# Writing a small transposed table to memory: 2048 four-byte pieces, or a turn on TensorE and 16 rows

## The chip, the cores and the metric

The kernel runs on one core of a Trainium2 chip. The metric is device time in microseconds (us) of one execution. Five engines work in parallel, each through its own list of instructions in order: TensorE (PE in the profile), VectorE (DVE), ScalarE (ACT), GpSimd (POOL) and SyncE (SP), which here issues most of the DMA transfers.

## The reference

Two layers of a diffusion backbone work on 512 latent tokens and 256 context tokens of 1024 channels, in 32-bit floats. A layer normalises its input, modulates it by a shift and a scale that depend on a conditioning vector, projects it, runs two attentions side by side (a neighbourhood attention and a grouped-query attention, 8 heads of 64 each), merges them through gates, projects once more, and adds the result to its input, multiplied by a third conditioning factor, the residual gate:

```python
mod_x = jax.nn.silu(c) @ w_ada + b_ada
shift_x, scale_x, gate_x = jnp.split(mod_x[:, None, :], 3, axis=-1)
mod_c = jax.nn.silu(c_ctx) @ w_ada + b_ada
shift_c, scale_c, gate_c = jnp.split(mod_c, 3)
hx = _rmsnorm(x, norm_g) * (1.0 + scale_x) + shift_x
hc = _rmsnorm(ctx, norm_g) * (1.0 + scale_c) + shift_c
...
out_x = _merge(a_att, b_att, a_z, b_z, g_a, g_b, w_o_a, w_o_b, w_out)
x_new = x + gate_x * out_x
if update_ctx:            # layer 0 only
    ...
    ctx = ctx + gate_c * out_c
```

This document is about how the 1024 values of `gate_x` (and, in layer 0, the 1024 of `gate_c`) travel from where they are computed to where they multiply.

## The kernel before

Tokens are worked in tiles of 128. Products are kept close to 32-bit accuracy by splitting both operands in a high and a low part and adding three products (`mm3`, lines 429 to 431: these three lines are most of PE's work). Weights come in as `raw` tiles of 128x512 (lines 397 and 411, issued by SyncE), ScalarE casts them to the high part `whi` (lines 399 and 414), and VectorE or GpSimd subtract to get the low part `wlo` (lines 402 and 416).

A layer goes through these stages: the projections for the neighbourhood attention (pool `cp0` or `cp1`), the neighbourhood attention (`na`), the projections for the grouped-query attention (`bp`), that attention (`gq`), and the merge with the output projection (`mrg`). While attention heads wait for their softmax, PE works on pieces of other projections from a list called `fill`: the paths through SiLU (`za`, lines 610 and 612), the merge gates and the first output projection.

In the grouped-query stage, head by head, `gq_scores` computes four blocks of 128 queries against 768 keys (lines 857 and 858), takes the maximum (VectorE, line 1127) and the exponential (ScalarE, line 1128), and then `turned` (line 795) casts the probabilities to a 16-bit high part `h` on ScalarE (line 798), subtracts for a low part on VectorE or GpSimd (line 799), and has SyncE issue a DMA transpose of both into `ht` (line 800). `gq_values` divides (lines 807 and 808), multiplies `ht` with the values (lines 1144 and 1145, all four blocks of the head at once) and hands the result to `head_out` (lines 791 to 793). `hilo` splits the gated results (lines 652 and 653).

The conditioning factors that are not needed at once are computed in the background, spread over the stages. `ada_steps` loads the weight columns as `rawb` tiles (line 288) and has VectorE form dot products into `asum` (line 295), one column of 128 channels at a time, for each of two halves of the conditioning vector. For the residual gates these are tiles 16 to 23; `gate_steps` (line 589) makes the list of them and puts `ada_gate` at its end. The list is run one step at a time between blocks of attention:

- Layer 0 has two conditioning vectors (latent and context, `nv` = 2). Its first half runs in the neighbourhood attention, its second half, with `ada_gate` at the end, in the grouped-query attention, one step after each block of queries (line 1130).
- Layer 1 has one (`nv` = 1). The whole list runs in the first projections, a few steps after each token tile (lines 735, 747 and 748).

`ada_gate` adds the two halves (line 304, tile `as`) and the bias (line 314, tile `ag`), halves the result (line 316) and stores it to a table in memory, `gd`, from line 317. In SBUF the values lie with the channel inside a block of 128 on the partitions and the block number along the row. In `gd` they lie as rows of 128 channels. At the start of the merge, line 1180 reads each vector back as one row of 1024, spread over all 128 partitions (`gate`), and line 1218 multiplies with it.

The order of the instructions on each engine is written by a planner that simulates the program with costs of its own and takes whatever it thinks is ready; only where `behind` (line 464) is used is an order fixed by hand. `turn` (line 516) and the divisions use the two PSUM buffers of kind `t`. In the attentions, `pool` is the pool of the stage (`att["p"]`; `Parts` puts two named tiles elsewhere), and `hp["p"]` in the projections.

Of the kernel before, what the change touches and what calls it, by code (L numbers as in the profile page):

```python
# [7 lines left out]
F32 = mybir.dt.float32  # L8
# [62 lines left out]
def hybrid_kernel(es: ExitStack, tc, x, ctx, cvec, w_ada, w_ada0, small, gvec, w_in, w_o_a, w_o_b, w_out,  # L71
                  bias_int, bias_edge, rope, ident_d, out):
    nc = tc.nc
    V, S, G, T = nc.vector, nc.scalar, nc.gpsimd, nc.tensor
# [10 lines left out]
    def nm(s):  # L85
        uid[0] += 1
        return f"{s}_{uid[0]}"
# [26 lines left out]
    def psw(n=512, kind="w"):  # L114
        if kind == "w":
            kind = "f" if pm["i"] % pm["n"] == 0 else "x"
            pm["i"] += 1
            if pm["i"] in pm["v_for"]:
                kind = "v"
        pool, cols = pm[kind]  # L120
        return pool.tile([128, cols], F32, tag=kind, name=nm("ps" + kind))[:, :n]
# [5 lines left out]
    gd = [drp.tile([16, 128], F32, name=f"gd{i}") for i in range(2)]  # L127
# [11 lines left out]
    ident = cp.tile([128, 128], F32, name="ident")  # L139
# [136 lines left out]
    def ada_steps(l, tiles, halves, nv, pool, queue=None):  # L276

        cb = {}

        def load(h):  # L280
            cb[h] = pool.tile([128, 2, 512], F32, tag="cb", name=nm("cb"), bufs=1)
            for v in range(nv):
                src = cd[8 * v + 4 * h:8 * v + 4 * h + 4].rearrange("k p -> (k p)").unsqueeze(0)
                nc.sync.dma_start(cb[h][:, v, :], src.to_broadcast([128, 512]))

        def load_tile(h, i):
            cb["w"] = pool.tile([128, 512], F32, tag="rawb", name=nm("rawb"), bufs=2)
            (queue or nc.sync).dma_start(cb["w"], w_ada[l, h, i])

        def dot(h, i, v):  # L290
            if v == 0:
                load_tile(h, i)
            w = cb["w"]
            o = w if v == nv - 1 else pool.tile([128, 512], BF16, tag="junk", name=nm("junk"), bufs=1)
            behind(ON_DVE, lambda: V.tensor_tensor_reduce(o, w, cb[h][:, v, :], 1.0, 0.0, ALU.mult, ALU.add,
                                                          asum[:, i, h, v:v + 1]))
        res = []
        for h in halves:
            res += [lambda h=h: load(h)] + [lambda h=h, i=i, v=v: dot(h, i, v) for i in tiles for v in range(nv)]
        return res  # L300

    def ada_sum(a, b, nv):
        s = sp.tile([128, b - a, 2], F32, tag="as", name=nm("as"), bufs=1)
        V.tensor_tensor(s[:, :, 0:nv], asum[:, a:b, 0, 0:nv], asum[:, a:b, 1, 0:nv], ALU.add)
        return s
# [1 line left out]
    def ada_mod(l):  # L307
        mod_finish(l, ada_sum(0, 16, 2).rearrange("p (a k) v -> p a k v", a=2), 0, 8)

    def ada_gate(l, nv):  # L310

        g = sp.tile([128, 2, 8], F32, tag="ag", name=nm("ag"), bufs=1)
        n = 8 * nv
        V.tensor_tensor(g[:, 0:nv], ada_sum(16, 24, nv)[:, :, 0:nv].rearrange("p k v -> p v k"),
                        gcol[:, 52 + 8 * l:60 + 8 * l].unsqueeze(1).to_broadcast([128, nv, 8]), ALU.add)
        V.tensor_scalar(g[:, 0:nv], g[:, 0:nv], 0.5, None, ALU.mult)
        nc.sync.dma_start(gd[l][0:n].rearrange("n p -> p n"), g[:, 0:nv].rearrange("p v k -> p (v k)"))


    def make_hx(l, t, xt, hx, pool):  # L320
# [259 lines left out]
    def layer(l, hx, nxt, start):  # L580
# [6 lines left out]
        nv = 2 if first else 1  # L587

        def gate_steps(halves, pool):
            return (ada_steps(l, range(16, 24), halves, nv, pool)  # L590
                    + ([lambda: ada_gate(l, nv)] if 1 in halves else []))
        gq = gcol[:, 48 + 2 * l:49 + 2 * l]
        gk = cp.tile([128, 1], F32, name=nm("gk"))

# [121 lines left out]
        else:  # L716
# [3 lines left out]
            for t in range(6):  # L720
                tok_proj(w, 512, a_hx, t, evac_na(kav, False, gk, 4))
            bg = gate_steps((0, 1), hp["p"])
            run(bg, 1)
        per_bg = -(-len(bg) // (3 + qt))
# [30 lines left out]
        if True:  # L755
# [266 lines left out]
            def values_of(dst, f, back=None):  # L1022
# [6 lines left out]
                return g  # L1029

            bg = gate_steps((0,), att["p"]) if first else []
            pipeline(fill, 9, na_first, values_of(za, na_values), bg=bg)

# [127 lines left out]
            def early():  # L1161

                for c in (1, 3):
# [4 lines left out]
            own = {"cb": vbig[:, 1152:2176].rearrange("p (v n) -> p v n", v=2),  # L1168
                   "junk": vbig[:, 2176:2432].bitcast(BF16)}
            bg = gate_steps((1,), Parts(att["p"], own)) if first else []  # L1170
            pipeline(fill, 8, gq_first, values_of(zb, gq_values, vs[:, 1:2]), early, bg)
            gq_es.close()
# [323 lines left out]
```

## Time and profile before

| | us |
|---|---|
| three runs | 1131.86 median, 1130.71 lowest, 1135.87 highest |
| the profiled execution | 1136.54 |
| its span, first to last instruction | 1134.8 |
| PE busy, matmuls | 1092.4 |
| VectorE, ScalarE, GpSimd busy | 765.3, 578.0, 490.5 |
| mean granted clock of PE | 0.989 of full |

The granted clock is the share of PE's full clock that the chip allows at that moment. Views of the profile used below: the page (busy times, and a table of DMA issues by kind with the median time to landing), the list of waits (who waited for whom: total, times, longest, in us), windows (busy time of each engine in a stretch, with clock and DMA rate), the timeline (start, length, engine, line, operation, with the idle time before it and what ended it in brackets), and the chain of work that ended last (start, length, what). An engine with a q behind its name is its instruction sequencer. A line such as L317 is a line of the kernel.

### The profile page before, as it was taken

The page shows a single profiled execution, that of the slowest core. Times are in us where ns is not written, and L with a number is a line of the kernel's source. Part 1 is how long each engine was busy: PE and PEld are TensorE (multiplying, and loading weights), DVE is VectorE, ACT ScalarE, POOL GpSimd, SP SyncE. Part 2 cuts the span into 40 slices and gives each one's busy share as a digit, 9 for nine tenths or more (in the row PEclk, how much of TensorE's full clock was granted, in tenths as well). Part 3 has the DMA queues.
Part 4 walks back from the last instruction along what each step waited for, and adds up shares of the span by engine and source line. Part 5 has one row for each costly group of instructions (what it writes and reads, how often), then busy time and mean ns, then how long its engine had stood idle before and what let it go on. Part 6 is the DMA issues. An engine that isn't in the chain of part 4 may idle for free.

```text
span 1134.8 us, 16867 instructions
## 1 busy us (share of the span) xinstructions
PE 1092.4 (96%) x5824; PEld 905.5 (80%) x5824; DVE 765.3 (67%) x1492; ACT 578.0 (51%) x1152; POOL 490.5 (43%) x405
## 2 busy tenths in 40 slices
PE   8999999999999999779999999999999999999998
PEld 5688888888988877557788888887888987777677
DVE  4666788888365478636567895357988765677473
ACT  6463266656333566555331275325666545776431
POOL 1044255654246245345521454335554563463530
PEclk9999999999999999989999999999999999999999
DMA  9454412233341597679733542453333236989742
GB/s 366 148 173 134 126 49 66 83 125 98 110 140 47 130 205 176 108 216 248 192 104 127 158 149 77 142 182 72 108 105 112 64 103 164 186 219 250 198 147 81
DMA packets 195278, 161.29 MB, mean 142 GB/s; under 512 B 119444, under 2 KB 161144, under 8 KB 193528
## 3 DMA queue, kind: packets, MB, share of 16 engines
q1 hardware_dynamic: 187856, 145.82, 47.2%
q0 software_dynamic: 2368, 7.87, 2.1%
q10 hardware_dynamic: 4968, 6.53, 1.7%
q8 instruction: 46, 0.75, 0.3%
q14 instruction: 40, 0.33, 0.1%
HBM read 115.58 MB, written 17.32 MB: 117 GB/s over the span
## 4 chain that ended last, share of the span: by engine, by line
PE 78%; DMA 6%; DVE 5%; issue 5%; POOL 3%; ACT 2%; SPq 1%; POOLq 0%; ACTq 0%; DVEq 0%
PE psx L431 11%; PE psx L430 11%; PE psx L429 11%; PE psf L429 9%; PE psf L430 8%; PE psf L431 8%; PE pst L775 2%; PE pss L951 2%; PE pss L857 2%; PE pss L858 2%; DMA raw<-in_w_in_dram 2%; DMA ht<-h 1%; PE pst L521 1%; PE pst L1144 1%; PE pst L1145 1%
## 5 line engine op out<-in xcount | busy, mean ns | idle before, releaser
L429 PE MATMUL psf<-hx,whi 128*128 128x512 f32 (+1 forms) x360 | 137.9, 383 | 4.1 <-ACT zt L610 2.5
L416 POOL TENSOR_TENSOR wlo<-raw,whi 128x512 fp32r<-128x512 f32 x70 | 98.0, 1405 | 94.4 <-ACT whi L414 64.3
L431 PE MATMUL psf<-hx,wlo 128*128 128x512 f32 (+1 forms) x360 | 135.8, 377 | 0.0
L430 PE MATMUL psf<-hx,whi 128*128 128x512 f32 (+1 forms) x360 | 135.2, 376 | 0.0
L429 PE MATMUL psx<-whi,hx 128*128 128x512 f32 (+1 forms) x328 | 120.7, 371 | 0.0
L430 PE MATMUL psx<-wlo,hx 128*128 128x512 f32 (+1 forms) x328 | 119.7, 366 | 0.0
L431 PE MATMUL psx<-whi,hx 128*128 128x512 f32 (+1 forms) x328 | 119.5, 365 | 0.0
L414 ACT CAST whi<-raw 128x512 fp32r<-128x512 f32 x136 | 82.5, 620 | 72.6 <-DMA raw<-in_w_in_dram 44.9
L402 POOL TENSOR_TENSOR wlo<-raw,whi 128x512 fp32r<-128x512 f32 x40 | 61.0, 1528 | 120.6 <-ACT whi L399 73.0
L799 POOL TENSOR_TENSOR h<-p,h 128x768 f16<-128x768 f32 (+1 forms) x40 | 64.9, 1626 | 99.7 <-ACT h L798 79.1
L399 ACT CAST whi<-raw 128x512 fp32r<-128x512 f32 x88 | 54.4, 623 | 100.4 <-PE psx L431 33.9
L500 POOL TENSOR_TENSOR ss<-ss,ehalf 128x8 f32<-128x8 f32 (+2 forms) x40 | 62.2, 1558 | 74.1 <-DVE ss L497 74.0
L416 DVE TENSOR_TENSOR wlo<-raw,whi 128x512 fp32r<-128x512 f32 x66 | 66.6, 1009 | 28.9 <-ACT whi L414 27.4
L1127 DVE CUSTOM_DVE_ANT_0 p<-pss,vb 128x768 f32<-128x768 f32 x64 | 60.2, 953 | 36.7 <-PE pss L858 19.9
L429 PEld LDWEIGHTS psf<-hx,whi 128*128 128x128 f32 x360 | 67.9, 189 | 16.1 <-ACT zt L610 3.6
L431 PEld LDWEIGHTS psf<-hx,wlo 128*128 128x128 f32 x360 | 67.8, 188 | 11.5
L430 PEld LDWEIGHTS psf<-hx,whi 128*128 128x128 f32 x360 | 67.9, 189 | 10.3
L1128 ACT ACTIVATE p<-pss,mx 128x768 f32<-128x768 f32 x64 | 57.5, 900 | 35.0 <-DVE mx L1127 31.5
L431 PEld LDWEIGHTS psx<-whi,hx 128*128 128x128 f32 x328 | 61.9, 189 | 10.0
L430 PEld LDWEIGHTS psx<-wlo,hx 128*128 128x128 f32 x328 | 62.0, 189 | 9.2
L429 PEld LDWEIGHTS psx<-whi,hx 128*128 128x128 f32 x328 | 61.7, 189 | 8.9
L429 PE MATMUL psx<-hx,whi 128*128 128x256 f32 (+1 forms) x208 | 68.1, 327 | 0.0
(359 smaller groups left out, 3097.5 us busy)
## 6 DMA issues: line engine op xcount, KB each, us to landing
raw<-in_w_in_dram SPq DMA_DIRECT2D x168, 256.0 KB, 2.9
rawb<-in_w_ada_dram SPq DMA_DIRECT2D x48, 256.0 KB, 2.8
raw<-in_w_out_dram SPq DMA_DIRECT2D x32, 256.0 KB, 3.1
tg<-gs SPq DMA_DIRECT2D x4, 1536.0 KB, 6.4
rawx<-in_w_ada_dram SPq DMA_DIRECT2D x4, 1024.0 KB, 13.3
rawy<-in_w_ada_dram SPq DMA_DIRECT2D x4, 1024.0 KB, 10.3
gs<-zt ACTq DMA_DIRECT2D x16, 256.0 KB, 2.1
raw<-in_w_o_a_dram SPq DMA_DIRECT2D x16, 256.0 KB, 3.4
```

The costliest lines, as they stand in the source:

```text
L399: S.copy(hi[:, :n], raw[:, :n])
L402: e.tensor_tensor(lo[:, :n], raw[:, :n], F(hi[:, :n]), ALU.subtract)
L414: S.copy(hi, raw)
L416: lo_eng(i).tensor_tensor(lo, raw, F(hi), ALU.subtract)
L429: T.matmul(ps, lhs[0], rhs[0], start=first, stop=False)
L430: T.matmul(ps, lhs[0], rhs[1], start=False, stop=False)
L431: T.matmul(ps, lhs[1], rhs[0], start=False, stop=last)
L500: G.tensor_tensor(ss, ss, ehalf[:, :n], ALU.pow)
L775: T.transpose(pt[:, c0:c0 + 128], src, ident)
L799: eng.tensor_tensor(h[:, 1], p[:, :n], h[:, 0], ALU.subtract)
L1127: V.tensor_tensor_reduce(p, pss, lift, -1.0, 3e38, ALU.add, ALU.min, mx[:, 0:1])
L1128: S.activation(p, pss, AF.Exp, bias=mx[:, 0:1], accum_out=r[:, i:i + 1])
```

## The change

Instead of writing `gd` straight from the tile `ag` through a transposed access pattern, in which neighbouring elements in memory come from different partitions (16 x 128 pieces of 4 bytes in layer 0, 8 x 128 in layer 1), `ada_gate` turns the tile on TensorE through a PSUM buffer of kind `t`, copies the 16 (or 8) rows of 128 to a small tile `agt` on ScalarE, and stores those rows, 512 bytes each. `ada_gate` is handed the pool in which `agt` lies.

```diff
-    def ada_gate(l, nv):
+    def ada_gate(l, nv, pool):
 
         g = sp.tile([128, 2, 8], F32, tag="ag", name=nm("ag"), bufs=1)
         n = 8 * nv
         V.tensor_tensor(g[:, 0:nv], ada_sum(16, 24, nv)[:, :, 0:nv].rearrange("p k v -> p v k"),
                         gcol[:, 52 + 8 * l:60 + 8 * l].unsqueeze(1).to_broadcast([128, nv, 8]), ALU.add)
         V.tensor_scalar(g[:, 0:nv], g[:, 0:nv], 0.5, None, ALU.mult)
-        nc.sync.dma_start(gd[l][0:n].rearrange("n p -> p n"), g[:, 0:nv].rearrange("p v k -> p (v k)"))
+        pt = psw(512, "t")
+        T.transpose(pt[0:n, 0:128], g[:, 0:nv].rearrange("p v k -> p (v k)"), ident)
+        gt = pool.tile([16, 128], F32, tag="agt", name=nm("agt"), bufs=1)
+        S.copy(gt[0:n], pt[0:n, 0:128])
+        nc.sync.dma_start(gd[l][0:n], gt[0:n])
...
         def gate_steps(halves, pool):
             return (ada_steps(l, range(16, 24), halves, nv, pool)
-                    + ([lambda: ada_gate(l, nv)] if 1 in halves else []))
+                    + ([lambda: ada_gate(l, nv, pool)] if 1 in halves else []))
```

## Prediction

> **What bounds the kernel now.** I read the page first, for the busiest engine and its idle total; then the list of PE's waits, to see which stall is long; then a table of short windows around that stall; then SyncE's own timeline and the chain of waits through it, for the cause; and last the same places in layer 1.
>
> ```profile
> span 1134.8 us, 16867 instructions
> PE 1092.4 (96%) x5824; PEld 905.5 (80%) x5824; DVE 765.3 (67%) x1492; ACT 578.0 (51%) x1152; POOL 490.5 (43%) x405
> ```
>
> TensorE (PE) is busy for 1092.4 of 1134.8 us. Only PE's 42.4 us of idle time, and time at a reduced clock, can be won without removing matmuls. The profiled execution took 1136.54 us, 1.74 more than its span.
>
> ```profile
> PE pst L1144 <- DMA ht<-h: 14.8, 3, 11.8
> 474.60 0.28 PE L858 MATMUL pss<-gk,qs 128*128 128x256 f32 x1
> 486.71 0.59 PE L1144 MATMUL pst<-ht,vb 128*128 128x512 f16 x1 [11.83 <-DMA ht<-h]
> ```
>
> One wait (total, times, longest, in us) is 11.8 us long: PE stops at 474.88 and resumes at 486.71 because a DMA transpose into `ht` is late. That is over a quarter of PE's idle time, in layer 0's grouped-query stage. The windows there (span, busy us of each engine, granted clock, DMA share, GB/s):
>
> ```profile
> core 0: us, PE busy (x) PEld busy (x) DVE busy (x) ACT busy (x) POOL busy (x), PEclk, DMA share, GB/s
> 465.00:467.00 2.00, 2.00 (x10) 1.68 (x9) 1.20 (x2) 1.95 (x4) 0.00 (x0) 1.00 1.15 299
> 470.00:475.00 5.00, 4.88 (x38) 4.50 (x36) 4.69 (x5) 2.55 (x7) 2.39 (x2) 1.00 0.21 12
> 475.00:477.00 2.00, 0.00 (x0) 0.00 (x0) 0.20 (x3) 0.00 (x0) 0.00 (x0) 1.00 0.16 12
> 479.00:480.00 1.00, 0.00 (x0) 0.00 (x0) 0.00 (x0) 0.00 (x0) 0.00 (x0) 0.66 0.70 119
> 480.00:484.00 4.00, 0.00 (x0) 0.00 (x0) 0.00 (x0) 1.41 (x4) 0.72 (x1) 0.50 1.22 264
> ```
>
> From 470 to 477 the DMA engines move 12 GB/s, then 264 once something has cleared. During the stall VectorE, ScalarE and GpSimd have almost nothing to do either, so the time isn't being used for something else that would be late next. PE's clock falls to half at about 479.3 (0.66 over that one microsecond), 4.4 us after PE stopped. SyncE (SPq) shows what the queue holds:
>
> ```profile
> 464.93 0.37 SPq L317 DMA_DIRECT2D gd<-ag  x1
> 465.58 2.23 SPq L411 DMA_DIRECT2D raw<-in_w_o_a_dram  x1
> 467.89 1.44 SPq L800 DMA_TRANSPOSE ht<-h  x1
> 469.39 14.94 SPq L800 DMA_TRANSPOSE ht<-h  x2
> L800 SPq DMA_TRANSPOSE ht<-h x64: 1273/1594/12456, 388.6 to 1060.1; - x64
> DMA to landing us min/median/max: 3.7/4.3/15.3
> 475.21 6.63 SPq L800
> 481.94 4.64 DMA ht<-h
> 487.30 0.43 PE pst L1145
> 489.77 0.22 PE pst L1145
> ```
>
> The store of the gate factors, L317, is issued at 464.93. Right behind it stand a weight load and three transposes of head 4. Issuing a transpose takes 1.59 us at the median of 64 and 12.456 at most; that maximum is the second of these three, from 469.39 to 481.84. The chain (start, length) runs through this blocked issue and then the ordinary landing of the third (4.64, median 4.3) to PE. The low rate begins behind the 2048-piece store, and the queue frees itself some 14 us after it.
>
> **The change part by part.** *The stall in layer 0.* Without the blocked queue, the last transpose goes out when its input is ready.
>
> ```profile
> 469.49 0.83 ACT L798 CAST h<-p 128x768 f16<-128x768 f32 x1
> 470.81 1.66 POOL L799 TENSOR_TENSOR h<-p,h 128x768 f16<-128x768 f32 x1
> ```
>
> That input ends at 472.47; add 4.3 for the landing and PE can start at 476.8, 1.9 us after it ran dry. So 11.8 − 1.9 = 9.9 us go, and a wait of 1.9 for the same transpose is what is late next. It is short of the 4.4 us after which the clock fell, so the reduced clock should go too: the seven matmuls from 486.71 to 489.77 take 3.06 us (0.43 and more each) and would take 7 × 0.22 = 1.54 at the rate of the next one. Gain 1.5; together 11.4.
>
> *Layer 1.*
>
> ```profile
> 767.69 0.38 SPq L317 DMA_DIRECT2D gd<-ag  x1
> raw<-in_w_in_dram SPq DMA_DIRECT2D x168, 256.0 KB, 2.9
> 772.23 9.72 DMA raw<-in_w_in_dram
> 784.02 0.50 PE L429 MATMUL psf<-hx,whi 128*128 128x512 f32 x1 [1.61 <-DVE za L612]
> SPq L317 <- DVE ag L316: 5.6, 1, 5.6
> ```
>
> The store of 1024 pieces leaves at 767.69. A weight load issued at 772.23 lands 9.72 us later, where 168 such loads have a median of 2.9. ScalarE's cast, the SiLU behind it and PE follow, and PE idles 1.61 us. PE had matmuls until then, so only this 1.6 is won. Half the pieces hold the queue about as long, so the hold isn't simply a price per piece; I do not need that price. Loads there that land at the median have 7 us of slack. Total gain: 13.0.
>
> *What is added.* In each layer: one turn of a 128x16 or 128x8 tile on PE, one copy out of PSUM on ScalarE, and a store that now waits for the copy.
>
> ```profile
> 768.55 0.44 PE pst L521 x4
> 469.10 0.37 ACT L791 COPY ho<-psv 64x256 f32<-64x256 f32 x1
> cd<-csl SPq DMA_DIRECT2D x1, 8.0 KB, 2.5
> 464.73 0.17 DVE L316 TENSOR_SCALAR ag<-ag 128x16 f32<-128x16 f32 x1
> 464.07 0.40 PE L429 MATMUL psf<-hx,whi 128*128 128x512 f32 x1
> 469.32 0.39 PE L431 MATMUL psf<-hx,wlo 128*128 128x512 f32 x1
> 768.59 0.60 ACT L610 ACTIVATE za<-psx 128x512 f32<-128x512 f32 x1 [4.75 <-PE psx L431]
> ```
>
> The turns: four 128x128 ones take 0.44, so 0.11 each, 0.2 for both, on the path because PE is. The copies: at most 0.37 each, the nearest row with more rows and columns. In layer 0 it sits on ScalarE ahead of the casts that feed the last transpose, so 0.4 counts; in layer 1 ScalarE had been idle 4.75 us, which hides it (if that cover is gone, another 0.4). The store itself has a twin: `cd<-csl` is also 16 rows of 512 bytes, 8 KB, and lands in 2.5 us. I take that over the 14 us of the pieces.
>
> The new waits. PE takes its instructions in a planned order, so the turn waits for `ag`, ready at 464.9; queued behind it is the fill piece that ran from 464.07 to 469.71, and a turn planned ahead of that piece would idle PE for 464.9 − 464.1 = 0.8 us. Planned inside it, nothing: I take the middle, 0.4. On ScalarE the copy waits for the turn, with the exponentials and casts of head 4 behind it. On SyncE the store waits for the copy, with one weight load and the three transposes behind it, and PE's L1144 waits for those. Taken with the turn inside the piece, the store leaves about a microsecond later than now and the first transpose, at 467.89 today, loses nothing. If the turn comes only after the piece, at 469.7, it holds copy and store: copy done at 470.1, then the load (0.4) and three transposes at about 1.4 each, the last issued at 473.7 and landed at 478.0. That is 1.2 more than the 476.8 above. If ScalarE stands still at the copy meanwhile, it is more (a rival below). In layer 1 loads of biases and weights stand behind the store, and by the 7 us of slack above a microsecond there is free. But SyncE came to that store 5.6 us before `ag` was ready; had the plan put the turn as early on PE, PE would idle up to 5.6 us. I take 0, because PE's transposes of that stretch (L521) run between pieces without such a wait, and keep 5.6 for the range.
>
> The PSUM ring `t` has two buffers and gets one more user in each layer; its neighbours are read out microseconds before they are needed again, so nothing is charged for it. The load that reads the factors back stands far off:
>
> ```profile
> L1180 SPq DMA_DIRECT2D gate<-gd x3: 382/383/422, 557.9 to 1069.1; - x3
> ```
>
> at 557.9, some 90 us behind the first store, hence no reader waits for the longer route.
>
> Sum: −11.4 − 1.6 + 0.2 + 0.4 + 0.4 = −12.0 us. Against the profiled 1136.54 that is 1124.5. That execution lies 4.7 above the median of the runs shown, and no row says where the 4.7 are: taken off the median, the result is 1119.9; if part of the 4.7 was a longer hold of the queue, the gain on the median is smaller. I set it one microsecond higher: 1121.
>
> A rule for weighing it: the Trainium skill, page "DMA: Bandwidth & Descriptors", section "Rules for kernel authors", says that a transfer with a non-contiguous last dimension becomes one descriptor per element, which by itself would agree with the trace's 14 us hold. The same page's section "Anatomy of one DMA" fits a DMA's time as 2.0 us plus its bytes over 436 GB/s, by which both forms of the 8 KB store cost an estimated 2.02 us; the change would then win nothing. The 12 GB/s behind the store speak for the first sentence, and the second is the third rival below.
>
> **The rivals.** *The turn holds ScalarE and SyncE (0.13).* If the copy is planned early on ScalarE and the turn late on PE, ScalarE stands from about 465 to 469.8, the casts of head 4 move back by some 4 us, the last input comes at 476.5 instead of 472.5, and PE waits 4 us longer, 5.9 in all, past the 4.4 at which the clock falls: 4.0 + 1.5 lost of the gain, 1126.5. At worst the turn comes last before PE runs dry: store at 475.5, last transpose issued at about 479 and landed at 483.4, a wait of 8.5 in place of 11.8: with layer 1's gain and the added work 3.3 + 1.6 − 1.0 = 3.9 us are won of 12.0, or 1121 + 8.1 = 1129. For it: PE is the fullest engine and fill matmuls are what it does when the turn becomes ready. Against it: in this stretch single matmuls of other tiles stand between those of a fill piece.
>
> *The order of everything behind it changes, to the worse (0.10).* The planner writes the order of all engines from its own costs, and two turns, two copies and a cheaper store change its times from 465 on. The place would be GpSimd's splits of the gated values (columns: start, length; in brackets the idle time before and its releaser):
>
> ```profile
> 503.30 7.60 POOL L653 TENSOR_TENSOR gal<-za,gah 128x768 fp32r<-128x768 f32 x4
> 507.49 0.79 PE L429 MATMUL psf<-gah,whi 128*128 128x512 f32 x1 [3.69 <-ACT zt L610]
> ```
>
> Four of them in a row hold the split of the next head's probabilities for 7.6 us, and PE idles 3.69 in that stretch. If a new order puts such a block in front of the transposes' inputs in later heads, each costs up to 7.6; two are 15.2, over the 12.0 won, which is where it decides against the change: 1121 + 15.2 = 1136, three 1144. For it: such blocks exist now. Against it: most other heads show no PE stall of that length, and a new order can as well dissolve this one.
>
> *The pieces aren't the cause (0.05).* If a store's time went by its bytes, the block would come from the weight loads and transposes themselves, it would stay, and the 1.0 of added work gives 1133. Against it: the other 63 transposes stand among the same loads and none took as long to issue.
>
> **How the numbers follow.** The forecast has 0.72, with a range of its own of 1113 (the 1.9 wait vanishes as well and a few microseconds of other waits with it) to 1126. A measurement of this kernel can tell about 0.5% from no change, 5.7 us: faster is under 1126.2, slower over 1137.5. Faster: 0.70 of the forecast and 0.05 of the first rival, 0.75. Same: 0.02 of the forecast, 0.08 of the first rival, 0.05 of the third and 0.02 of the second, 0.17. Slower: 0.08 of the second. The range, 1113 to 1132, takes in the forecast but for its tails and nearly all of the first rival; it leaves out the other two and some 0.04 of the forecast, just under 0.2.
>
> **What would show it.** Right: no transpose in layer 0 takes over about 3 us to issue, the wait of L1144 on `ht` falls from 11.8 us to 1 to 3, no window of half clock around it, and the first weight load behind the layer 1 store lands in 3 to 4 us. The store lands in about 2.5. Wrong in size: ScalarE idle for microseconds ahead of the new copy, or PE idle ahead of the turn. Wrong altogether: a long issue of a transpose behind the new store, or new PE waits of several microseconds after 500 in places where there were none.

## The result, and the profile after

| | before | after |
|---|---|---|
| median of eight runs each, us | 1132.88 | 1126.91 |
| lowest and highest, us | 1130.71, 1135.87 | 1123.76, 1129.11 |
| the profiled execution, us (span) | 1136.54 (1134.8) | 1127.56 (1125.6) |

The changed kernel takes 0.9945 of the time before, with an interval of 0.993 to 0.996: some 6 us less, where 12 were forecast (1121, range 1113 to 1132). The two profiled executions lie 9.0 us apart; the one of before took 3.7 us more than its median, the one of after 0.7.

The page after:

```profile
span 1125.6 us, 16862 instructions
PE 1093.3 (97%) x5826; PEld 905.3 (80%) x5826; DVE 774.7 (69%) x1492; ACT 579.0 (51%) x1154; POOL 490.6 (44%) x405
```

Its list of PE's waits:

```profile
PE psv L811 <- DVE ho L796: 5.8, 1, 5.8
PE psf L433 <- ACT zt L614: 4.0, 5, 1.6
...
PE pst L1148 <- DMA ht<-h: 2.3, 3, 1.4
```

SyncE's timeline around the first store (start, length; the length of a group includes the gaps between its instructions):

```profile
463.22 2.52 SPq L415 DMA_DIRECT2D raw<-in_w_o_a_dram  x3
465.83 6.65 SPq L804 DMA_TRANSPOSE ht<-h  x3
472.57 0.60 SPq L321 DMA_DIRECT2D gd<-agt  x1
```

Behind line 317 the numbers are four higher than before: L1148 is the old L1144, L811 the old L807. PE is as busy as it was (1093.3 against 1092.4); what went is idle time. The wait for `ht`, 11.8 us long before, has a longest of 1.4 us anywhere. At the top stands a wait that the kernel before doesn't have, 5.8 us on VectorE. The three transposes of head 4 now stand ahead of the store in SyncE's queue and go out in 6.65 us together. The windows of the same stretch and of what follows it (span, busy us of each engine with its instructions, granted clock, DMA share, GB/s):

```profile
465.00:485.00 20.00, 20.00 (x113) 15.61 (x112) 12.05 (x24) 12.96 (x27) 6.51 (x5) 1.00 0.79 168
485.00:490.00 5.00, 5.00 (x41) 4.65 (x39) 2.91 (x6) 4.98 (x9) 2.55 (x2) 1.00 0.73 161
490.00:495.00 5.00, 2.78 (x12) 1.94 (x11) 4.94 (x5) 4.88 (x12) 5.00 (x4) 0.82 0.93 369
495.00:500.00 5.00, 1.35 (x5) 0.86 (x3) 5.00 (x1) 1.83 (x4) 4.91 (x4) 0.84 1.05 314
500.00:505.00 5.00, 2.85 (x9) 2.47 (x10) 4.06 (x7) 0.00 (x0) 1.85 (x2) 0.50 0.11 25
```

From 465 to 490, where the kernel before stood still for 11.8 us, PE is busy throughout at full clock and the DMA engines move 161 to 168 GB/s. Then from 490 to 505 it is busy for 6.98 of 15 us, the last five of them at half clock. Between 495 and 500 VectorE's five busy microseconds are a single instruction. The timeline there, and behind it the group of all instructions of that line and shape (shortest, median and longest in ns):

```profile
491.54 7.15 POOL L657 TENSOR_TENSOR gal<-za,gah 128x768 fp32r<-128x768 f32 x4
492.20 8.26 DVE L420 TENSOR_TENSOR wlo<-raw,whi 128x512 fp32r<-128x512 f32 x1
498.63 1.29 POOL L420 TENSOR_TENSOR wlo<-raw,whi 128x512 fp32r<-128x512 f32 x1
501.67 0.42 DVE L796 TENSOR_TENSOR ho<-psv,ho 64x256 f32<-64x256 f32 x1
502.15 0.69 PE L811 MATMUL psv<-ident,r 128*128 128x128 f32 x2 [5.80 <-DVE ho L796]
```

```profile
L420 DVE TENSOR_TENSOR wlo<-raw,whi x66: 666/694/8258, 97.4 to 1053.8; 128x512 fp32r<-128x512 f32 x66
```

The subtraction that makes `wlo` takes 0.694 us at the median of 66 and 8.258 here. It begins 0.66 us behind the first of GpSimd's four subtractions and ends at 500.46, 0.54 us after GpSimd has run out of work (498.63 + 1.29 = 499.92). Queued behind it on VectorE is `ho`, and PE waits for that. The Trainium skill, page "SBUF — State Buffer", section "SBUF: two separate sides", says that VectorE operations with two SBUF inputs and GpSimd operations that read SBUF lock each other out of a port pair for a whole instruction. The trace agrees that VectorE was held, but not for one instruction: it was held through five GpSimd instructions in a row, each 1.3 to 1.8 us long, 7.6 us in all. That need not be so. In the kernel before, the same subtraction starts in the middle of the same block (503.30 to 510.90) and gets through in 1.50 us:

```profile
505.93 1.50 DVE L416 TENSOR_TENSOR wlo<-raw,whi 128x512 fp32r<-128x512 f32 x1 [1.60 <-ACT whi L414]
```

What decides between the two is not shown by any run here.

To compare kernels at equal places I use two anchors: the first multiplication by the factors (line 1218 before, 1222 after), in the merge of layer 0, and the last one, near the end; the two times at the end of the rows are the starts of the first and the last. Of before, then of after:

```profile
L1218 DVE TENSOR_TENSOR t<-psx,gate x16: 676/686/692, 610.2 to 1124.8; 128x512 f32<-128x512 f32 x16
```

```profile
L1222 DVE TENSOR_TENSOR t<-psx,gate x16: 677/685/692, 601.8 to 1115.7; 128x512 f32<-128x512 f32 x16
```

At the first the changed kernel is 8.4 us ahead, at the last 9.1. Layer 0 decides.

### The profile page after: what moved, and what is told of

Read it like the earlier page. It is cut to its first block, busy times and chain, and to the rows that moved or that the text cites. A ratio compares the mean times of both kernels' runs of the same rounds, so it can differ in the third digit from the quotient of the medians.

```text
span 1125.6 us, 16862 instructions
## 1 busy us (share of the span) xinstructions
PE 1093.3 (97%) x5826; PEld 905.3 (80%) x5826; DVE 774.7 (69%) x1492; ACT 579.0 (51%) x1154; POOL 490.6 (44%) x405
## 4 chain that ended last, share of the span: by engine, by line
PE 38%; issue 4%; DVE 3%; DMA 3%; POOL 2%; ACT 1%; SPq 1%; POOLq 0%; ACTq 0%
PE psx L435 6%; PE psx L433 6%; PE psx L434 6%; PE psf L433 4%; PE psf L434 4%; PE psf L435 4%; PE pss L955 1%; PE pss L861 1%; POOL wlo L406 1%; PE pss L862 1%; PE pst L779 1%; PE pst L1148 1%; DMA raw<-in_w_o_a_dram 1%; PE pst L1149 1%; DMA raw<-in_w_in_dram 1%
## 5 line engine op out<-in xcount | busy, mean ns | idle before, releaser
L420 DVE TENSOR_TENSOR wlo<-raw,whi 128x512 fp32r<-128x512 f32 x66 | 73.6, 1115 | 30.6 <-ACT whi L418 29.0
L435 PE MATMUL psx<-hx,wlo 128*128 128x256 f32 (+1 forms) x208 | 68.0, 327 | 0.0
```

The costliest lines, as they stand in the source:

```text
L420: lo_eng(i).tensor_tensor(lo, raw, F(hi), ALU.subtract)
L435: T.matmul(ps, lhs[1], rhs[0], start=False, stop=last)
```

## The experiments

Theory A: the pieces hold the DMA queue, and the forecast's missing half is lost to the planner's new order. Theory B: the gain comes from the new order, and the form of the store matters little. Theory C: the hold is worth only the 6 us that were measured. The last two runs ask something else: whether the traced execution of before was held longer than most. In brackets behind a ratio stands its 95% interval. Ratios are to the kernel before on the same chip.

**128 rows, no turn.** The store without TensorE: `gd` takes the layout of `ag`, and the factors are read back with a stride. The planned order of PE, VectorE, ScalarE and GpSimd is that of before.

```diff
-    gd = [drp.tile([16, 128], F32, name=f"gd{i}") for i in range(2)]
+    gd = [drp.tile([128, 16 >> i], F32, name=f"gd{i}") for i in range(2)]
...
-        nc.sync.dma_start(gd[l][0:n].rearrange("n p -> p n"), g[:, 0:nv].rearrange("p v k -> p (v k)"))
+        nc.sync.dma_start(gd[l], g[:, 0:nv].rearrange("p v k -> p (v k)"))
...
-                    V.tensor_tensor(t1, ps, gv[:, 0 if t < 4 else 1, cs], ALU.mult)
+                    V.tensor_tensor(blocks(t1), blocks(ps), gate(0 if t < 4 else 1, 512 * n, 512), ALU.mult)
```

> The kernel before, but the table is stored as it lies in SBUF: 128 rows of 64 bytes in layer 0 and of 32 bytes in layer 1, no turn and no copy; it is read back as one row, and the multiply picks its elements with a stride. The planned order of the kernel before stays on PE, ScalarE, VectorE and GpSimd. Theory A (the pieces of 4 bytes held SyncE's queue; the rest of the forecast gain was lost because the new plan brings a new stall at the next head): the 11.8 us wait of L1144 falls to about 2, PE waits nowhere anew, the span falls by about 12, and the time is below that of the changed kernel, ratio to before about 0.991. Theory B (the plan is where the gain came from, the store's form matters little): the wait stays near 11.8 and the ratio is 1.00. Theory C (the hold is worth only the 6 us measured): ratio 0.9945, as the changed kernel.

It took 1124.66 us, 0.9914 [0.9894, 0.9934], below the changed kernel's. Its timeline of SyncE and PE, and the group of the multiplications:

```profile
464.44 0.34 SPq L317 DMA_DIRECT2D gd<-ag  x1
465.06 0.37 SPq L411 DMA_DIRECT2D raw<-in_w_o_a_dram  x1
465.52 7.89 SPq L800 DMA_TRANSPOSE ht<-h  x3
475.83 0.38 PE L1144 MATMUL pst<-ht,vb 128*128 128x512 f16 x1 [1.44 <-DMA ht<-h]
```

```profile
L1223 DVE TENSOR_TENSOR t<-psx,gate x16: 1001/1054/1130, 597.9 to 1113.1; 128x512 f32<-128x512 f32 x16
```

The queue is as before, with the store first, and the wait is 1.44 us where it was 11.83. The clock stays full there. This is the change as the prediction's first part imagined it, where 1.9 us were to be left over. The first anchor comes 12.3 us earlier, the last 11.7. The strided read costs 1.05 in place of 0.685 us in each multiplication, and nothing on the whole: PE does not wait for them. So the pieces are the cause: theory B falls, and with the time below that of the changed kernel theory C too.

**The old store from ScalarE's queue.** Is it SyncE's queue that is held, or the DMA engines?

```diff
-        nc.sync.dma_start(gd[l][0:n].rearrange("n p -> p n"), g[:, 0:nv].rearrange("p v k -> p (v k)"))
+        S.dma_start(gd[l][0:n].rearrange("n p -> p n"), g[:, 0:nv].rearrange("p v k -> p (v k)"))
```

> The kernel before, with the same store in pieces of 4 bytes issued by ScalarE's queue instead of SyncE's; PE's order is unchanged. If only the ring of SyncE is held, the transposes of head 4 issue in about 1.5 us each, L1144 waits about 2 us and the ratio is near 0.991. If the DMA engines themselves are held, the transposes wait behind the pieces as before: L1144 waits 8 to 12 us and the ratio is 0.998 to 1.003.

1130.99 us, 0.9972 [0.9961, 0.9983]. Its timeline of SyncE and PE, and the row of layer 0's store in the table of DMA issues (the last number is the time from issue to landing):

```profile
465.91 14.77 SPq L800 DMA_TRANSPOSE ht<-h  x3
483.06 0.58 PE L1144 MATMUL pst<-ht,vb 128*128 128x512 f16 x1 [8.34 <-DMA ht<-h]
```

```profile
gd<-ag ACTq DMA_DIRECT2D x1, 8.0 KB, 13.7
```

The pieces take 13.7 us to land. The transposes of the other queue are held nearly as long: the wait is 8.3 us. The hold is mostly in what the two queues share. What that is stays open. From 470 to 475 the DMA engines count as busy here (a share of 1.29) at only 37 GB/s, whereas in the trace of before their share in that window is 0.21:

```profile
470.00:475.00 5.00, 4.72 (x37) 4.34 (x35) 3.93 (x8) 2.34 (x7) 2.90 (x2) 1.00 1.29 37
```

**The store of layer 0 done twice**, the second time into a table that nobody reads.

```diff
+        if l == 0:
+            nc.sync.dma_start(gd[2][0:n].rearrange("n p -> p n"), g[:, 0:nv].rearrange("p v k -> p (v k)"))
```

> The kernel before, with layer 0's store in 2048 pieces of 4 bytes done twice, the second time to a table that nobody reads; the order of PE, ScalarE, VectorE and GpSimd is unchanged. Theory A: the hold doubles, L1144 waits about 24 us in place of 11.8, span +12 to +14 and ratio about 1.011. Theory B: no change, ratio 1.00. If the hold is one fixed delay behind any store of this kind, not a cost per piece (layer 1's half as many pieces held as long): +0 to +3.

1138.99 us, 1.004 [1.0025, 1.0056]; the wait is 17.4 us long. PE's waits, and SyncE's timeline:

```profile
PE pst L1146 <- DMA ht<-h: 20.0, 3, 17.4
```

```profile
467.70 13.52 SPq L802 DMA_TRANSPOSE ht<-h  x1
481.94 8.18 SPq L802 DMA_TRANSPOSE ht<-h  x2
```

Twice the pieces cost 5.6 us more of waiting than in the profile of before, not 11.8 more, and the ratio is below the 1.011 that a doubled hold was expected to give. That pieces cost is confirmed; that the hold grows in proportion to them is not. The trace also counts the pieces: it has 197342 DMA packets where that of before has 195278, 2064 more for 2048 more pieces, all of them under 512 bytes.

**The turn, but the pieces stored.** PE's and ScalarE's planned order is that of the changed kernel.

```diff
-        nc.sync.dma_start(gd[l][0:n], gt[0:n])
+        nc.sync.dma_start(gd[l][0:n].rearrange("n p -> p n"), g[:, 0:nv].rearrange("p v k -> p (v k)"))
```

> The changed kernel with its turn and its copy, but the store again goes from the tile before the turn in pieces of 4 bytes (the copied rows are used by nobody); the order on PE and ScalarE is that of the changed kernel. Theory A: the hold is back behind the store, some 13 us; in this order PE needs the transposes of head 4 only at 482, so part of it is covered: L1148 waits 3 to 8 us there, ratio to before 0.998 to 1.002. Theory B (the plan makes the gain): as the changed kernel, 0.9945.

1135.19 us, 1.0005 [0.9993, 1.0017]. The new plan and the added work alone bring nothing; with that plan the form of the store is worth 1.0005 − 0.9945, 0.6%, some 7 us, and with the plan of before 0.7 to 0.9% (the 128 rows, here and below). SyncE's timeline has the block again; the longest of PE's waits stand behind it:

```profile
467.90 13.49 SPq L804 DMA_TRANSPOSE ht<-h  x2
```

```profile
PE pss L861 <- ACT p L880: 6.7, 2, 5.5
PE pst L1148 <- DVE ho L796: 3.0, 1, 3.0
```

In this plan the readers of `ht` stand behind other work, and PE's long waits are 5.5 and 3.0 us in other places of the same stretch: from 470 to 520 it is busy for 36.53 us, where the changed kernel has 41.08.

**The turn in another PSUM buffer.** In the changed kernel's plan the division and the value products of head 3, which use the kind `t`, moved from about 460 to behind the turn at 468. With a wide buffer the turn doesn't take one of that kind.

```diff
-        pt = psw(512, "t")
+        pt = psw(512)
```

> The changed kernel, with the turn through a PSUM buffer of the kinds that the projections use (kind f in layer 0) instead of kind t. In the planned order head 3's products with the values then stay where they were in the kernel before. Theory A (the turn's place in the ring of two t buffers pushed them, and with that brought the wait of 5.8 us at head 5): no VectorE subtraction of 8 us there, PE's longest wait in layer 0's grouped-query stage is 3.7 as in the kernel before, span about 1123 and ratio to before 0.990 to 0.993. Rival (any new plan loses a few us, whatever the buffer): ratio 0.994 to 0.997.

1131.66 us, 0.9973 [0.9962, 0.9984]: slower than the changed kernel, where 0.990 to 0.993 was expected. Head 3's value products are back at 458 to 461, so in layer 0 the `t` buffer does set their place. The turn itself now comes at 493.6, behind PE's wait of 3.7 us for `zt` that the kernel before has as well. The first anchor comes at 594.8, the earliest of all kernels here and 7.0 us ahead of the changed one. But the last comes at 1117.7, 2.0 us behind the changed kernel, and one new wait is on the way, where layer 1 normalises its heads (PE's waits, then a window):

```profile
PE psf L433 <- DVE y L513: 5.5, 1, 5.5
```

```profile
700.00:760.00 60.00, 54.52 (x239) 44.48 (x238) 25.46 (x55) 16.14 (x29) 14.23 (x10) 0.94 0.46 137
```

The changed kernel is busy for all of those 60 us. The buffer alone, in both layers, gives one plan for another. The edit is also less clean than it looks: where there are several wide buffers, `psw` deals them out in turn by a counter (lines 114 to 120), so one more taker can shift the buffers of the products behind it.

**GpSimd's four subtractions on VectorE.**

```diff
-            hilo(za, gated["a"], range(4))
+            hilo(za, gated["a"], range(4), V)
```

> The changed kernel, with the low parts of the gated neighbourhood results (the four subtractions of 128x768 that GpSimd does in a row from 491.5 to 498.7) on VectorE. Theory A2 (GpSimd's run of subtractions stops VectorE in the middle of a subtraction, 8.26 us instead of 0.69, and that makes the wait of 5.8): no subtraction on VectorE over 2 us in that stage, the wait of 5.8 gone, 3 to 6 us won on the changed kernel, ratio to before 0.989 to 0.992. Rival (VectorE was waiting for its own inputs, or becomes the bound with 4 us more work): the wait stays or moves to VectorE, ratio 0.994 or above.

1127.51 us, 0.9944 [0.993, 0.9958], the time of the changed kernel. The wait of 5.8 us is gone, the `wlo` subtraction takes at most 1.94 us, yet nothing is won, where 3 to 6 us were expected. The windows of the changed kernel, then of this one:

```profile
485.00:520.00 35.00, 26.08 (x136) 20.66 (x134) 26.13 (x33) 19.05 (x38) 17.25 (x12) 0.85 0.83 252
520.00:550.00 30.00, 28.51 (x154) 21.04 (x155) 16.00 (x31) 16.90 (x32) 15.55 (x12) 1.00 0.76 158
650.00:700.00 50.00, 50.00 (x250) 41.56 (x249) 34.86 (x53) 33.32 (x78) 25.82 (x23) 1.00 0.31 100
```

```profile
485.00:520.00 35.00, 30.29 (x171) 24.16 (x170) 27.87 (x48) 23.22 (x44) 16.29 (x12) 0.95 0.90 241
520.00:550.00 30.00, 26.03 (x137) 19.56 (x136) 15.45 (x23) 13.48 (x25) 16.26 (x12) 0.94 0.69 173
650.00:700.00 50.00, 47.92 (x232) 37.95 (x231) 31.90 (x50) 30.70 (x73) 21.67 (x18) 1.00 0.30 89
```

4.2 us of PE work more in the first stretch, 2.5 and 2.1 less in the two others: the gain is given back by 700. So the block does cause the 5.8 us wait, since the wait goes with it, but its removal changes the plan once more.

**Both of these mends with others.** The same edit on the 128-row kernel, and with the wide buffer.

> The kernel with 128 rows stored as they lie (first experiment) and the four subtractions of the gated neighbourhood results on VectorE. If the 3.7 us wait of PE for the tanh behind that block, and the half clock around it, come from GpSimd's 7.6 us: another 3 to 5 us off the first experiment, ratio to before 0.987 to 0.989. If the block is hidden there: 0.991 as the first experiment.

> The changed kernel with the turn through the other PSUM kind and the four subtractions on VectorE. If both losses are separate and each is mended: ratio to before 0.986 to 0.989, below each alone. If they are the same loss: 0.990 to 0.992, as the better of the two.

1125.44 us, 0.9923 [0.9907, 0.9938], no better than 128 rows alone: its longest PE wait, 3.7 us for `zt`, stays, so GpSimd's block isn't what makes that one. And 1133.04 us, 0.999 [0.9978, 1.0002], with the layer 1 wait of the wide buffer (5.4 us) again, where 0.986 to 0.992 was expected. The mends don't add up.

**The changed kernel and the 128 rows side by side.**

> The changed kernel once more, beside the 128-row version on the same chip. If the new order of the plan costs some 3 us (the theory), it comes to 0.993 to 0.996 of the kernel before, and 2 to 5 us above the 128-row version. If the two are the same and the distance between them was chance, both come to about 0.993.

> The 128-row store with the order of the kernel before. The theory: 0.990 to 0.993 of the kernel before, below the changed kernel. If the distance was chance: about 0.993, as the changed kernel.

1127.43 us, 0.995 [0.9931, 0.9968], and 1124.92 us, 0.993 [0.9909, 0.9951]. The distance is 2.5 us. The first medians, 1126.91 and 1124.66, lie 2.3 us apart, but they were taken beside different runs of the kernel before (1132.88 and 1134.45); by their ratios it is some 3.5. The intervals of the ratios overlap, so the distance is not certain, but it had the same sign both times, and the traces agree on its place. The windows of the changed kernel's second trace, and of the two of the 128 rows:

```profile
485.00:520.00 35.00, 26.13 (x136) 20.49 (x133) 26.04 (x33) 18.44 (x37) 17.21 (x12) 0.80 0.83 237
```

```profile
485.00:520.00 35.00, 29.43 (x164) 23.79 (x162) 19.57 (x38) 21.03 (x41) 21.34 (x15) 0.90 0.98 284
```

```profile
485.00:520.00 35.00, 29.33 (x160) 23.71 (x159) 19.25 (x39) 21.89 (x43) 22.11 (x16) 0.90 0.96 283
```

PE works 3.2 to 3.4 us less in these 35 us in both traces of the changed kernel, at a lower mean clock; the stretched subtraction repeats (8.24 us). With the plan of before, GpSimd's block is there as well, and a wait of 3.7 us for `zt` as before, but not the one of 5.8: the subtraction beside the block takes 1.50 us there.

**The kernel before, traced twice more**, to see whether the profiled execution on which the sum was made is typical.

> The kernel before once more, for its trace. If the profiled execution on which the sum was made held the queue longer than most do (the theory, since removing the hold is worth 8 to 10 us on the medians and 11.5 in the profile), the wait of L1144 for ht comes to 8 to 11 us here and the wait in layer 1 to 0 to 1.6. If the holds are always of that length (the rival), 11.8 and 1.6 come again within 0.5, and the excess lies elsewhere.

> As the run before it, a third trace of the kernel before: the theory expects 8 to 11 us and 0 to 1.6, and that the two traces differ; the rival 11.8 and 1.6.

Executions of 1135.05 and 1134.63 us, with spans of 1133.3 and 1132.9. PE's waits, in that order, and a window of the second:

```profile
PE pst L1144 <- DMA ht<-h: 13.7, 3, 10.9
```

```profile
PE pst L1144 <- DMA ht<-h: 13.0, 3, 10.2
```

```profile
760.00:800.00 40.00, 40.00 (x191) 33.24 (x191) 33.61 (x66) 23.17 (x44) 22.30 (x17) 1.00 0.33 83
```

The wait is 0.9 and 1.6 us shorter, and in neither trace does PE wait in layer 1 behind the store of 1024 pieces: the window is that stretch. The store of layer 0 lands in 13.1 and 12.8 us. So the traced execution was held longer than the two others, whose spans are 1.5 and 1.9 us shorter; 11.8 and 1.6 were the values of one execution.

## Why the prediction was right, and where its sizes were off

The forecast was faster, 1121 us within 1113 to 1132; the result is 1126.91. The sign and the cause held, and half of the 12.0 in the sum came. That the number lies well inside the range is in part luck: the forecast alone was given only up to 1126, and 1126.91 stands next to the 1126.5 of the first rival, which cost nothing here. By its steps:

- **The cause** was read rightly: the store of pieces holds the DMA queue, the transposes are late, PE waits. The same plan with 128 rows leaves 1.44 us of the 11.83.
- **Layer 0, 11.4.** The chain and what is late next were right; the size was that of one execution. With the waits of the other two traces, 10.2 and 10.9, the same working gives 9.8 to 10.5. The prediction had named this doubt. One reading in it was wrong without harm: the 4.4 us after which the clock fell were one case and no threshold. In the same trace PE runs dry at 503.80 (507.49 − 3.69), and the mean clock of the window behind it puts the fall to half at about 506.6, 2.8 us later. In the changed kernel the clock falls at about 493.2, where PE's waits had been 1.6 and 0.6 us. A remaining wait of 1.9 us was thus no safeguard; with the 1.44 that remained in the 128 rows the clock stayed full. Of before, then of after:

```profile
504.00:508.00 4.00, 0.51 (x1) 0.50 (x2) 1.83 (x2) 3.94 (x7) 4.00 (x3) 0.83 1.00 424
```

```profile
493.00:494.00 1.00, 0.58 (x1) 0.50 (x2) 1.00 (x1) 0.97 (x5) 1.00 (x2) 0.58 0.99 418
```

- **Layer 1, 1.6.** This term failed. It was a real wait in a single execution, but two more traces of the same kernel don't have it. The hold itself is there in all three: ScalarE waits up to 5.6, 3.0 and 3.3 us for the weight loads behind the store, and at most 0.3 with 128 rows (below, the third trace of before and then the 128 rows). PE had enough other work to cover it in two of three. Together the removal is worth some 9 to 10 us, not 13.0; the runs of the 128 rows show 1134.45 − 1124.66 = 9.8, and 1133.76 − 1124.92 = 8.8 the second time.

```profile
ACT whi L414 <- DMA raw<-in_w_in_dram: 3.7, 2, 3.3
```

```profile
ACT whi L414 <- DMA raw<-in_w_in_dram: 0.3, 1, 0.3
```

- **What is added, 1.0.** Each direct term was right or too high. PE never waited for `ag`: in layer 0 the turn came at 468.07, 2.4 us after it, with no idle time before it. The copy took 0.25 us (at most 0.37 was said):

```profile
L320 ACT COPY agt<-pst x2: 249/252/255, 469.6 to 758.5; 16x128 f32<-16x128 f32 x1, 8x128 f32<-8x128 f32 x1
468.07 0.27 PE L318 MATMUL pst<-ident,ag 128*16 128x128 f32 x1
```

- **The PSUM ring, at nothing.** This step failed, and it was the wrong question. No wait for a `t` buffer shows, but the planner puts head 3's values behind the turn because of it, and the heads behind that come in another order. Against the 128 rows, which add no operations, the added part costs 2.5 us on the medians side by side, not 1.0, and it lies between 485 and 520.
- **The second rival** had this place and this block of GpSimd's, but another victim: it feared that GpSimd's own split of the probabilities would come late, for 7.6 us each time. What was held is a subtraction on VectorE, once, and the price against the order of before is some 3.3 us of PE's work in that stretch, since the old order had idle time there too. The idle 3.69 us that the prediction read beside the block are not the block's doing: they stay when the block runs on VectorE. A new order did cost time beside the forecast, not in its place, and the sign stayed.
- **The first rival**, the turn holding ScalarE and SyncE, did not occur in layer 0. SyncE's order changed instead: the store stands behind the three transposes, so that its wait for the copy holds none of them. In layer 1 ScalarE did stand still at the copy for 4.1 us (12.2 with the wide buffer), which had been named as a sign of a wrong size. In the changed kernel PE is busy for all of the 60 us from 700, so it cost nothing there:

```profile
758.52 0.26 ACT L320 COPY agt<-pst 8x128 f32<-8x128 f32 x1 [4.09 <-PE pst L318]
```

- **The signs that were named.** PE's wait for `ht`, the full clock around it and the loads behind the layer 1 store (2.9 us to landing) came as said. "No transpose in layer 0 takes over about 3 us to issue" was wrong as a sign: two take 7.13 and 6.01, at 489.49 and 508.32, each behind two loads of `tg`, and PE does not wait for the first there. The 2.5 us to the store's landing are not borne out: the trace of after doesn't show it, and with the wide buffer, where the same 16 rows leave at 494 and 499, they take 8.9 and 5.5. As 128 rows it is 3.4 us in layer 0. Nothing waits for it. New PE waits of several microseconds after 500 were named as a sign that all is wrong; there is one, it ends at 502, and it took a part of the gain.

So 13.0 − 1.0 = 12.0 was in fact 8.8 − 2.5 = 6.3 in the runs side by side. Both terms are taken by way of the 128 rows, so that their sum is the measured gain by construction and no check of its own. What stays open: what the pieces hold, why 2048 pieces more add some 6 us to the wait when the first 2048 make 10 to 12, and which decision of the planner gives the gain of each mend back; the traces show only where it goes.

## What to carry to other kernels

A store whose neighbouring elements in memory come from different partitions is dear for what stands behind it, in other queues too: give it rows, and if the reader can stand a stride, change the layout of the table rather than the data, since an edit that adds no operations leaves the order of all the rest as it was. A stall that is read from one trace is the stall of one execution: trace the kernel again before adding up terms of a microsecond or two. Where a planner writes the order, an added operation's price can be mostly the new order, and a local wait that is then mended can come back elsewhere.

## What the runs showed of the hardware

- The windows of before behind the store, from 467 to 477, show 12 to 41 GB/s in stretches of 3 to 4 us, though 8 KB would be nothing at any of the rates seen: the pieces take 12.8 to 13.9 us to land in the four runs whose tables show it. 128 rows of 64 bytes land in 3.1 to 3.5. Of the two rules of the Trainium skill, page "DMA: Bandwidth & Descriptors", that the prediction weighed, the one of "Rules for kernel authors" is one descriptor per element for a non-contiguous last dimension. The traces agree, with 2064 more packets for the 2048 pieces of the second store. The same page of the Trainium skill gives the fit of "Anatomy of one DMA" for DMAs issued through GpSimd, and this store is SyncE's. The 2.02 us estimated by it are far from what the pieces take.
- Transposes issued by SyncE are held by pieces that ScalarE's queue issued (a wait of 8.3 us against 10.2 to 11.8).
- One VectorE subtraction of 128x512 took 8.26 us beside GpSimd's subtractions (median 0.694), 8.24 in the second trace; in the kernel before, beside the same block, 1.50. The longest where the block runs on VectorE is 1.94.
